# A Strassen-Winograd matmul on one core: the first region's last turn as quarter products, measures later, b21's stores behind VectorE

## The chip, the core and the metric

The kernel runs on one core of a Trainium2 chip. A core has TensorE (matrix products into PSUM, eight banks of 128 x 512 float32), VectorE, ScalarE, GpSimd (POOL) and SyncE (SP), each with an instruction queue of its own that runs in order; they meet through semaphores. Data moves between HBM and SBUF by DMA; DMAs are issued here from the queues of SP, ScalarE and POOL. POOL's loads also turn float32 into float16 on the way. The metric is the device time of one execution in microseconds (us); the time given for a kernel is the median over its runs.

## The reference

```python
def setup_inputs():
    m, k, n = 4096, 4096, 4096
    return {
        "a": np.random.randn(m, k).astype(np.float32),
        "b": np.random.randn(k, n).astype(np.float32),
        "alpha": np.float32(0.01),
    }

def reference(a, b, alpha):
    x = np.matmul(a, b)
    return np.where(x > 0, x, alpha * x)
```

## The kernel before

**Tiling.** The output is 16 regions of 1024 x 1024: row group g and column block j, each from 0 to 3. A region's rows are halves h = 0, 1 of 512 rows (MT = 4 tiles of 128), its columns halves nt = 0, 1 of 512. K = 4096 is four units u of 1024 (KC = 8 chunks of 128); units 0, 1 are the first half of K, units 2, 3 the second. So a region multiplies a 2 x 2 block matrix a11, a12, a21, a22 by b11, b12, b21, b22. Every element of a and b is rounded to float16.

**A region after the first** (the loop at L819, in the order of `regions`: (0, 1), (0, 2), (0, 3), then (1, 2), (1, 0), (1, 3), (1, 1), and so on) takes Winograd's seven products instead of eight. `PRODUCTS` (L684) lists their operands: a11 b11, a12 b21, s2 t2, s3 t3, s1 t1, a22 (b21 less t2), s4 b22. The sums s1 to s4 of a (`sum_a`, L598) and the sums t of b (`b_sum`, L618) are made by VectorE in float16. A plain product is 64 matmuls of 128 x 512 (`product`, L838); it goes through k first, so that it reads the first unit of a half before the second. The result of product 0 in banks `y` is copied by ScalarE into banks `z` (L1258); product 1 is added into `z`, product 2 into `y`, product 3 goes into new banks.

**Quarters.** In later groups some products are themselves taken with seven products of quarters: `quarter_product` (L781) is 16 matmuls of 256 columns. Their sums of quarters are made by `sums_of_a` and `sums_of_b` on VectorE. Where two results share the start of a sum, ScalarE copies the bank that holds it to another one.

**The first region** (0, 0) is plain: eight steps of 64 matmuls, in turns by `TURNS` (L35), `[[0], [0, 1], [1, 2, 3], [2, 3]]`: half h = 0 with unit 0, half 1 with units 0, 1, half 0 with units 1, 2, 3, and last half 1 with units 2, 3. Each step `i` of the loop at L464 fetches what the next step needs, runs its matmuls into eight banks, turns the next pieces of a (VectorE transposes, L143), and, at a turn's end, adds the banks to `part[h]` in SBUF (`spill`, L322). `leave_first` (L333) applies the leaky step and stores. `at[0, 0, 0]`, the first unit of a, is brought in by TensorE transposes and copies (L380 to L387), and is laid out plainly; all other a tiles hold pairs of chunks.

**What stands around the change, in the order of the program.** At step 5's end VectorE makes the last turn's a22 (eight transposes) and the spills of `part[0]`, then four leaky steps, which let SP store `part[0]`. The loads of the next region's b11 and b12 are issued by POOL at step 5. In the loop for region (0, 1): POOL's loads of b21, b22 (L1197), POOL's stores of `part[1]`, VectorE's s1 and s2, product 0, copies of `y` to `z`, four b sums (L1276, L1279), the end of a measure, `keep_half` (SP stores the float16 b21 for later groups), s3, product 1.

**Buffers.** The pool `x` has three slots, through which pass in turn the first loads, `room`, `part[0]`, `part[1]`, then s1, s2 of region (0, 1); a new tile waits until all readers and writers of the slot's last tile are through. `b21` and the like have two slots each (two units), `a16` three.

**Measures** (`Measure`, L222) collect sums of squares of a and b by row and column for a check of the scale at the end: ScalarE squares four pieces of 2048 (L237), VectorE adds and folds them (L246 to L271). In the kernel before, the measure of a21 and those of the first columns' b21 and b22 are taken in the first region's last turn.

**What b is kept.** A b unit that a later group needs again is stored in float16 (`kept_half`) and loaded from there by SP (L561). The order on each queue is that of the program (`manual_schedule`, L88).

Of the kernel before, what the change touches and what calls it, by code (L numbers as in the profile page):

```python
# [8 lines left out]
P = 128  # L9
# [28 lines left out]
OTHERS = (0, 3)  # L38
KEPT_T = {CACHED: 1, 0: 2, 3: 2}


# [8 lines left out]
def kernel(  # L50
# [154 lines left out]

    def plain(t):
        return t.rearrange("p c m e -> p (c m e)").rearrange("p (c m) -> p c m", c=KC)

    def a_cols(t, c, mt, is_plain=False):
        rows = slice(mt * P, (mt + 1) * P)  # L210
        return plain(t)[:, c, rows] if is_plain else t[:, c // 2, rows, c % 2]

# [59 lines left out]

    class MeasureFirst(Measure):


        def end(self):
            for pairs, n in ((False, 0), (True, 2)):
                if n:
                    self.square(3)
                total = self.held[n]  # L280
                nc.vector.tensor_add(total, total, self.held[n + 1])
                fold(self.which, total, self.held[n + 1], pairs, 2.0)

    def halves(t):
# [4 lines left out]
    def mm(ps, h, u, mt, nt, c, first, last):  # L289
        nc.tensor.matmul(  # L290
            ps, a_cols(at[0, h, u], c, mt, (h, u) == (0, 0)), bt[0, u, nt][:, c, :],
            start=first, stop=last,
        )
# [39 lines left out]
    def leave_first(h, mt):  # L333
        kept = part[h][:, mt, :]
        leaky(kept)
        row = (h * MT + mt) * P
        if h == 0:
            nc.sync.dma_start(out[row:row + P, :2 * NT], kept)
        else:
            stores.append((out[row:row + P, :2 * NT], kept))  # L340

# [24 lines left out]
    def turn_a(i, r, tiles):  # L366
        k = slice(r * rw, (r + 1) * rw)
        shared = r and tiles == 1
        if shared and i == MT - 1:
            turned = both.pop()  # L370
        else:
            tag = "ps7" if r else f"ps{4 + i}"
            turned = psum_pool.tile([P, per, 2 if r else 1, P], DT, name="turned", tag=tag)
        if shared and i < MT - 1:
            both.append(turned)
        cols = a_rounded[:, :, k].rearrange("m t (p c) -> m t c p", c=per)
        for t in range(tiles):
# [9 lines left out]
        copy(to, turned)  # L387
# [31 lines left out]
    for n, (what, i, *more) in enumerate(order):  # L419
# [22 lines left out]
    room = x_pool.tile([P, 4, KC // 2 * RM], BF16, name="room", tag="x")  # L442
    part[0] = x_pool.tile([P, MT, 2 * NT], FP32, name="part", tag="x")
# [12 lines left out]
    for fetch in fetches[2]:  # L456
# [4 lines left out]
        Measure(1, halves(bt[0, 0, nt]) + halves(bt[0, 1, nt]), False, places)  # L461
        for nt, places in enumerate((room, c_rooms))]

    for i in range(1, len(steps)):  # L464
        t, h, u, first, last = steps[i]
# [24 lines left out]
        for g, (todo, leaves) in enumerate(groups):  # L490
            for mt, c in todo:
                for nt in range(2):
                    mm(banks[mt, nt], h, u, mt, nt, c, first and c == 0, last and c == KC - 1)
            if i == 5 and g > 1:
                spill(t, h, leaves, banks)
            for piece, turn in enumerate(following):
                if where[piece] == g:
                    turn()
            if leaves is not None and (i != 5 or g == 1):
                spill(t, h, leaves, banks)  # L500
            if leaves is not None and t and i != 5:
                leave_first(h, leaves)
# [9 lines left out]
        if i == 5:  # L512
            first_measure = Measure(0, halves(at[0, 1, 0]) + halves(at[0, 1, 1]), True, room)
            first_measure.begin()
            last_columns = [
                Measure(1, halves(bt[0, 2, nt]) + halves(bt[0, 3, nt]), False, places)
                for nt, places in enumerate((room, c_rooms))]
            for n in range(4):
                last_columns[1].square(n)
        if i == 6:  # L520
            first_measure.end()
            for n in range(4):
                last_columns[0].square(n)


    last_columns[0].end()

# [20 lines left out]
    def fetch_unit(i, u, nt, later=False):  # L548
# [9 lines left out]
        elif g and j == CACHED:  # L558
            nc.sync.dma_start(t, rows_of(kept[nt], u, 0, KC, True))
        elif half and (g and j == LAST or g > 1 and j in OTHERS):  # L560
            nc.sync.dma_start(t.rearrange("p c n -> p (c n)"), kept_half[j][u - 2, nt])  # L561
# [11 lines left out]
    whole_s = {}  # L573
    first_a = at[0, 0, 0]

    def flat(t):
        if t is first_a:
            return plain(t).rearrange("p (c e) m -> p c m e", e=2)
        return t.rearrange("p c m e -> p (c m e)")

    def like(t, other):

        return t if other is first_a else t.rearrange("p c m e -> p (c m e)")

    def a_sum(to, x0, x1, op):
        if x0 is first_a or x1 is first_a:
            f = lambda t: flat(t) if t is first_a else t
        else:
            f = flat
        nc.vector.tensor_tensor(f(to), f(x0), f(x1), op)  # L590
# [31 lines left out]
    def measure(i, which, x, y):  # L622
# [5 lines left out]
        parts = halves(tiles[0]) + halves(tiles[1])  # L628
        if tiles[0] is first_a:
            return MeasureFirst(which, parts, None)  # L630
        return Measure(which, parts, not which)
# [15 lines left out]
    def judge(line):  # L647
# [40 lines left out]

    HALF = NT // 2
    QUARTER = KC * HALF  # L690
    kept_s2 = dram_pool.tile([2, P, KC * RM], DT, name="kept_s2")
# [32 lines left out]

    def sums_of_a(g, name, room, some=(1, 2, 3, 4), made=None):

# [13 lines left out]
        make(2, 1, (0, 0), SUB)  # L740
        make(3, (0, 0), (1, 0), SUB)
        make(4, (0, 1), 2, SUB)

# [69 lines left out]
    def next_a(g, h, half):  # L813
        made = [p for k in range(2) for p in pieces_a(g, h, 2 * half + k)]
        return made

    in_quarters = False
    Y, Z = [4, 5, 6, 7], [0, 1, 2, 3]
    for i, (g, j) in enumerate(regions):  # L819
# [12 lines left out]

        def keep_half(some=(0, 1)):
            for nt in some:
                for k in ks:
                    nc.sync.dma_start(kept_half[j][k, nt], B(1, nt, k).rearrange("p c n -> p (c n)"))

        def product(n, banks, first):  # L838
# [23 lines left out]
            for mt, k, c in order:  # L862
                t = operand(g, name, k)
                nc.tensor.matmul(  # L864
                    banks[mt], a_cols(t, c, mt, t is first_a), B(half, nt, k)[:, c, :],
                    start=first and (k, c) == todo[0], stop=(k, c) == todo[-1], skip_group_check=not first,
                )
# [327 lines left out]
        if i == 0:  # L1195
# [4 lines left out]
            sum_a(g, "s1")  # L1200
            sum_a(g, "s2")
        coming = {}
        if turning:
# [52 lines left out]
        if not in_first:  # L1256
            for mt in range(MT):
                nc.scalar.copy(z[mt], y[mt])  # L1258
        if second_of_group:
            sums_of_a(g, "s1", new_a16)  # L1260
# [55 lines left out]
        if final:  # L1316
            good = next(judged)
        if (g, j) == (0, LAST):
            keep_half((1,))
        for k in [] if in_fourth else ks[1:] if turning and g else ks:  # L1320
# [16 lines left out]
        if in_fourth:  # L1337
            s5[3] = t[:, 3]
            load_sums("s1", s5, (3,))
            if g == 1 and j in OTHERS:  # L1340
                keep_half((1,))
        if turning and g:
# [132 lines left out]
        if not in_quarters:  # L1475
# [4 lines left out]
            else:  # L1480
                add(u2[::-1], z[::-1])
        if turning:

# [116 lines left out]
```

## Time and profile before

| what | value |
|---|---|
| median of 3 runs | 1523.87 us (1522.62 to 1524.34) |
| profiled execution | 1520.24 us |
| its span, first to last instruction | 1518.4 us |
| mean granted TensorE clock | 0.998 |
| DMA queue of POOL's loads (q0) | 45.1% of 16 engines' span |
| chain that ended last, TensorE's lines | L787 28%, L864 21%, L845 9% |

All times in a profile's rows are us from the span's start. A row of a timeline has its start, its length, the engine, the line and operation, written tile and read tiles, the shape and how many were merged; in brackets stands the idle time before it and what ended it. PE is TensorE's matmuls, PEld its weight loads, DVE VectorE, ACT ScalarE; a queue that issues a DMA has a q behind its name. The length of a merged row of matmuls counts the pipeline's depth once, so products are best measured from start to start.

### The profile page before, as it was taken

How to read it: one execution, taken by the hardware profiler on the slowest of the kernel's cores; microseconds unless marked ns; L12 is line 12 of the kernel's file. 1: busy time of each engine (PE TensorE's matmuls, PEld its weight loads, DVE VectorE, ACT ScalarE, POOL GpSimd, SP SyncE). 2: the span in 40 equal slices, each digit the busy share in tenths (PEclk: the TensorE clock that was granted, in tenths of full speed). 3: DMA queues.
4: the chain of work that ended last, by engine and by line, in shares of the span. 5: the costliest groups of instructions: out<-in, count | busy, mean ns of one | idle time of the engine just before them, and what ended most of it. 6: DMA issues, size and time to landing. Idle time of an engine off the chain costs nothing.

```text
span 1518.4 us, 24421 instructions
## 1 busy us (share of the span) xinstructions
PE 1507.9 (99%) x9883; PEld 965.8 (64%) x9883; DVE 1200.9 (79%) x1250; ACT 524.6 (35%) x906; POOL 252.2 (17%) x418
## 2 busy tenths in 40 slices
PE   9999999999999999999999999999999999999998
PEld 4444444444445667485544688888454488888887
DVE  4588966786696597697779698987887876998797
ACT  2441435647411123225671122323574112242322
POOL 5632110134201102012330101000331000100000
PEclk9999999999999999999999999999999999999999
DMA  9999697899889999999898989979989697987845
GB/s 245 188 219 259 151 278 212 129 220 192 202 347 228 299 293 296 282 289 300 199 246 344 261 315 257 345 246 316 242 215 306 258 278 278 242 291 188 348 154 183
DMA packets 193965, 384.97 MB, mean 254 GB/s; under 512 B 17585, under 2 KB 126385, under 8 KB 178738
## 3 DMA queue, kind: packets, MB, share of 16 engines
q0 software_dynamic: 115584, 108.03, 45.1%
q1 hardware_dynamic: 71058, 245.53, 43.1%
q10 hardware_dynamic: 7200, 29.76, 5.0%
q8 instruction: 79, 1.29, 0.3%
q14 instruction: 44, 0.36, 0.1%
HBM read 359.66 MB, written 129.50 MB: 322 GB/s over the span
## 4 chain that ended last, share of the span: by engine, by line
PE 58%; DVE 0%; issue 0%
PE ps L787 28%; PE ps L864 21%; PE ps L845 9%; DVE c L1146 0%; DVE b L620 0%; DVE c L320 0%
## 5 line engine op out<-in xcount | busy, mean ns | idle before, releaser
L864 PE MATMUL ps<-b,a 128*128 128x512 f16 x1984 | 433.3, 380 | 2.2 <-DVE a L590 2.2
L864 PEld LDWEIGHTS <-a 128*128 128x128 f16 x1984 | 194.4, 98 | 237.0 <-DVE a L590 2.7
L864 PE MATMUL ps<-b,s 128*128 128x512 f16 x1472 | 321.5, 379 | 0.5 <-DVE b L620 0.5
L864 PEld LDWEIGHTS <-s 128*128 128x128 f16 x1472 | 144.1, 98 | 173.9 <-issue 0.8
L564 POOL DMA_DIRECT2D b<-in_b_dram x120 | 88.9, 746 | 860.9 <-PE ps L787 282.6
L787 PEld LDWEIGHTS <-q 128*128 128x128 f16 x2192 | 214.1, 98 | 25.8 <-issue 0.4
L620 DVE TENSOR_TENSOR b<-b 128x4096 f16<-128x4096 f16 x82 | 185.8, 2285 | 42.5 <-DMA b<-in_b_dram 32.6
L887 ACT COPY c<-ps 128x512 f32<-128x512 f32 x164 | 86.2, 595 | 294.3 <-PE ps L864 157.0
L143 DVE STREAM_TRANSPOSE a<-a 128x512 uint32<-128x512 uint32 (+2 forms) x120 | 127.0, 1105 | 65.1 <-DMA a<-in_a_dram 64.6
L134 POOL DMA_DIRECT2D a<-in_a_dram x252 | 137.4, 552 | 246.7 <-ACT junk L639 74.9
L787 PEld LDWEIGHTS <-a 128*128 128x128 f16 x1440 | 140.9, 98 | 17.4
L320 DVE SCALAR_TENSOR_TENSOR c<-c 128x1024 f32<-128x1024 f32 (+2 forms) x123 | 141.8, 1190 | 8.9 <-ACT c L887 8.6
L639 ACT ACTIVATE junk<-a 128x512 bf16<-128x512 f16 x192 | 121.2, 631 | 69.9 <-DMA a<-in_a_dram 64.7
L787 PE MATMUL ps<-b,q 128*128 128x256 f16 x1088 | 128.1, 273 | 0.0
L237 ACT ACTIVATE sq<-b 128x2048 bf16<-128x2048 f16 x56 | 104.0, 1911 | 59.6 <-DVE sq L246 53.5
L787 PE MATMUL ps<-q,q 128*128 128x256 f16 x1024 | 119.0, 273 | 0.0
L290 PE MATMUL ps<-b,a 128*128 128x512 f16 x512 | 112.2, 379 | 0.3
L787 PE MATMUL ps<-b,a 128*128 128x256 f16 x912 | 107.4, 273 | 0.0
L787 PEld LDWEIGHTS <-s 128*128 128x128 f16 x960 | 93.9, 98 | 11.4
L290 PEld LDWEIGHTS <-a 128*128 128x128 f16 x512 | 49.7, 98 | 60.6 <-issue 1.4
L892 DVE TENSOR_TENSOR c<-ps,c 128x512 f32<-128x512 f32 x76 | 47.0, 679 | 30.4 <-PE ps L864 30.4
L845 PE MATMUL ps<-b,a 128*128 128x256 f16 x640 | 70.7, 273 | 0.0
(148 smaller groups left out, 1386.5 us busy)
## 6 DMA issues: line engine op xcount, KB each, us to landing
b<-in_b_dram POOLq DMA_DIRECT2D x128, 512.0 KB, 13.1
out_dram<-c SPq DMA_DIRECT2D x118, 512.0 KB, 8.0
a<-in_a_dram POOLq DMA_DIRECT2D x244, 128.0 KB, 5.5
b<-kept_half SPq DMA_DIRECT2D x28, 1024.0 KB, 12.4
b<-kept SPq DMA_DIRECT2D x20, 1024.0 KB, 8.4
q<-kept_qs ACTq DMA_DIRECT2D x40, 512.0 KB, 7.6
s<-kept_s SPq DMA_DIRECT2D x18, 1024.0 KB, 7.1
q<-kept_qs SPq DMA_DIRECT2D x28, 512.0 KB, 6.8
```

The costliest lines, as they stand in the source:

```text
L134: nc.gpsimd.dma_start(a16[32 * q:32 * q + 32], src.rearrange("(g i) w -> i g w", i=32))
L143: nc.vector.transpose(part.rearrange("p c m e -> p c (m e)").bitcast(U32) .rearrange("p c (g i) -> p g c i", i=32), src[:, :, i * n:(i + 1 ...
L237: nc.scalar.activation(to, self.parts[n], SQUARE)
L290: nc.tensor.matmul(ps, a_cols(at[0, h, u], c, mt, (h, u) == (0, 0)), bt[0, u, nt][:, c, :], start=first, stop=last,)
L320: nc.vector.scalar_tensor_tensor(t, t, alpha, t, op0=MULT, op1=MAX if alpha <= 1 else MIN)
L564: nc.gpsimd.dma_start(t[:, c:c + 4, :], b_rows(j, u, c, 4, nt, g > 0))
L620: nc.vector.tensor_tensor(f(to), f(x0), f(x1), op)
L639: nc.scalar.activation(junk, piece[:, q, :], SQUARE, accum_out=to[:, 4 * n + q:4 * n + q + 1])
L787: nc.tensor.matmul(to[m], xq[:, c // 2, rows, c % 2], yq[:, c, :], start=first and c == 0 and m < banks, stop=c == KC - 1, skip_group_chec ...
L845: nc.tensor.matmul(to, a_cols(operand(g, name, k), c, q // 2 * 2 + m), B(half, nt, k)[:, c, q % 2 * HALF:(q % 2 + 1) * HALF], start=False, ...
L864: nc.tensor.matmul(banks[mt], a_cols(t, c, mt, t is first_a), B(half, nt, k)[:, c, :], start=first and (k, c) == todo[0], stop=(k, c) == t ...
L887: nc.scalar.copy(to, bank)
```

## The change

The first region's last turn (steps 6 and 7) is taken out of the loop and written as two products of quarters, one for each nt, interleaved (`leave_in_quarters`). The sums of b21's quarters for nt = 0 are made at step 4's end, in `room`. In each set, the product of a22's last quarter by t4 needs no sum of a22 and goes ahead of those that do. `part[1]` gets the blocks by additions from PSUM; the leaky steps of both parts stand at the end, `part[0]`'s between the additions of the two nt.

```diff
+KEPT_IN = {(LAST, 0): 0, (LAST, 1): 0, (0, 0): 1, (0, 1): 1, (3, 0): 1, (3, 1): 0}
...
-    for i in range(1, len(steps)):
+    for i in range(1, len(steps) - last_turn):
...
-            if i == 5 and g > 1:
+            if i == 5 and 1 < g < MT:
                 spill(t, h, leaves, banks)
...
-        if i == 5:
-            for mt in range(MT):
-                leave_first(h, mt)
...
+            q = quarters_of_first(0)
+            f = lambda n: t_of_b21[n].rearrange("p (c n) -> p c n", n=HALF)
+            nc.vector.tensor_tensor(f(3), q[1, 1], q[0, 1], SUB)
+            nc.vector.tensor_tensor(f(2), f(3), q[0, 0], ADD)
+            nc.vector.tensor_tensor(f(4), q[1, 0], f(2), SUB)
...
+    def leave_in_quarters():
...
+        chain, one, other, shared, fourth = [new_bank(0), new_bank(2)], [new_bank(1), new_bank(3)], [], [], []
+        for nt in range(2):
+            quarter_product(x[0, 0], b[nt][0, 0], into(chain[nt]), True)
+            nc.scalar.copy(one[nt], chain[nt])
+        for nt in range(2):
+            quarter_product(x[0, 1], b[nt][1, 0], into(one[nt]))
+        fourth.append(new_bank(4))
+        quarter_product(x[1, 1], t(0, 4), into(fourth[0]), True)
+        tt(fx(1), xf[1, 0], xf[1, 1], ADD)
+        tt(fx(2), fx(1), xf[0, 0], SUB)
+        more(0, 0, 0, one[0])
+        tt(t(0, 1), b[0][1, 1], t(0, 2), SUB)
+        quarter_product(sx(2), t(0, 2), into(chain[0]))
+        other.append(new_bank(5))
+        nc.scalar.copy(other[0], chain[0])
+        shared.append(new_bank(1))
+        quarter_product(sx(1), t(0, 1), into(shared[0]), True)
+        tt(fx(3), xf[0, 0], xf[1, 0], SUB)
+        quarter_product(sx(3), t(0, 3), into(chain[0]))
+        tt(fx(4), xf[0, 1], fx(2), SUB)
+        quarter_product(sx(4), b[0][1, 1], into(other[0]))
+        tt(t(1, 3), b[1][1, 1], b[1][0, 1], SUB)
+        new_t(2, t(1, 3), b[1][0, 0], ADD)
+        quarter_product(sx(2), t(1, 2), into(chain[1]))
+        spill(2, 0, MT - 1, banks)
+        other.append(new_bank(6))
+        nc.scalar.copy(other[1], chain[1])
+        new_t(1, b[1][1, 1], t(1, 2), SUB)
+        shared.append(new_bank(7))
+        quarter_product(sx(1), t(1, 1), into(shared[1]), True)
+        more(1, 0, 0, one[1])
+        fourth.append(new_bank(3))
+        quarter_product(sx(3), t(1, 3), into(chain[1]))
+        nc.scalar.copy(fourth[1], chain[1])
+        quarter_product(sx(4), b[1][1, 1], into(other[1]))
+        new_t(4, b[1][1, 0], t(1, 2), SUB)
+        quarter_product(x[1, 1], t(1, 4), into(fourth[1]))
+        for nt in range(2):
+            more(nt, 1, 1, chain[nt])
+            for r in (1, 0):
+                more(nt, r, 1, shared[nt])
+            if nt == 0:
+                more(nt, 1, 0, chain[nt])
+            more(nt, 0, 1, other[nt])
+            more(nt, 1, 0, fourth[nt])
+            if nt == 0:
+                for mt in range(MT):
+                    leave_first(0, mt)
+        for mt in range(MT):
+            leaky(part[1][:, mt, :])
+            row = (MT + mt) * P
+            stores.append((out[row:row + P, :2 * NT], part[1][:, mt, :]))
...
-    Y, Z = [4, 5, 6, 7], [0, 1, 2, 3]
+    Y, Z = [2, 3, 6, 7], [0, 1, 4, 5]
```

Here `more` is one VectorE addition of a bank (128 x 512) to a block of `part[1]`, `tt` a VectorE operation on two tensors of 128 x 2048, `new_t` the same into a new slot of `a16`.

The measures move: a21's begins in region (0, 1) ahead of product 0 and ends behind the b sums; the first columns' b21 is measured in region (1, 0), ahead of its products, and their b22 in (3, 0).

```diff
     EARLY = {
-        (1, 3): [B11], (1, 1): [B11], (2, 3): [B21], (2, 1): [B12], (3, 1): [B21],
+        (1, 0): [B21], (1, 3): [B11], (1, 1): [B11], (2, 3): [B21], (2, 1): [B12], (3, 1): [B21],
     }
+    IN_C = (3, 0)
...
+            first_measure = Measure(0, halves(at[0, 1, 0]) + halves(at[0, 1, 1]), True)
+            first_measure.begin()
...
+        in_c = (g, j) == IN_C
+        if in_c:
+            m = measure(i, *B22)
+            m.room = [c_pool.tile([P, 2048], BF16, name="sq", tag=f"c{n}") for n in (side, side, 1 - side, 1 - side)]
+            for n in range(4):
+                m.square(n)
+        if second_of_group:
+            in_other = lambda n: c_pool.tile([P, QUARTER], DT, name="sums", tag=f"c{1 - side}") if n == 4 else new_a16()
+            sums_of_a(g, "s1", in_other if g == 1 else new_a16, m.end if in_c else None)
```

The stores of b for later groups follow a table, with b22 of column block 3 stored in group 0 instead of loaded again in group 1. In group 0, b21's stores get a one-column copy on VectorE in front of them.

```diff
-        def keep_half(some=(0, 1)):
-            for nt in some:
-                for k in ks:
-                    nc.sync.dma_start(kept_half[j][k, nt], B(1, nt, k).rearrange("p c n -> p (c n)"))
+        def keep_half(nt, behind=False):
+            for k in ks if KEPT_IN.get((j, nt)) == g else ():
+                t = B(1, nt, k).rearrange("p c n -> p (c n)")
+                if behind:
+                    nc.vector.tensor_copy(t[:, :1], t[:, :1])
+                nc.sync.dma_start(kept_half[j][k, nt], t)
...
         if i == 0:
-            last_columns[1].end()
+            first_measure.end()
...
-        if g == 1 and j in OTHERS or (g, j) == (0, LAST):
-            keep_half((0,))
+        keep_half(0, not g)
         note_rows()
         if first_of_group:
             sum_a(g, "s3")
...
         product(1, z, False)
...
+        if not g and i:
+            keep_half(1)
```

The first unit of a gets the layout of the others: its copies out of PSUM write pairs of chunks, and the plain layout's special cases (`plain`, `flat`, `like`, `MeasureFirst`) go.

```diff
-        to = plain(a0)[:, r * per:(r + 1) * per, first * P:(i + tiles) * P]
-        turned = turned.rearrange("p c t m -> p c (t m)")
+        to = a0[:, r * per // 2:(r + 1) * per // 2, first * P:(i + tiles) * P, :].rearrange("p c m e -> p c e m")
+        turned = turned.rearrange("p (c e) t m -> p c e (t m)", e=2)
```

More of the change, by code (lines that the diff above doesn't have):

```diff
@@ L271, in fold @@
             nc.vector.tensor_tensor(stats[:, n, which], stats[:, n, which], r, op)
[L273 to L282, printed above, removed]
     def halves(t):
@@ L336, in leave_first @@
         row = (h * MT + mt) * P
[L337 to L340, printed above, removed]
+        nc.sync.dma_start(out[row:row + P, :2 * NT], kept)
     runs = RUNS[0]
@@ L573 @@
     whole_s = {}
[L574 to L583, printed above, removed]
     def a_sum(to, x0, x1, op):
[L586 to L589, printed above, removed]
+        f = lambda t: t.rearrange("p c m e -> p (c m e)")
         nc.vector.tensor_tensor(f(to), f(x0), f(x1), op)
@@ L723, in sums_of_b, with sums_of_a @@
             tt(f(1), y[1, 1], f(2), SUB)
-    def sums_of_a(g, name, room, some=(1, 2, 3, 4), made=None):
+    def sums_of_a(g, name, room, ahead_of_4=None, some=(1, 2, 3, 4), made=None):
         x = {key: q.rearrange("p c m e -> p c (m e)") for key, q in quarters_of_a(g, name).items()}
@@ L815, in next_a, with t, new_t, more @@
         return made
+    def leave_in_quarters():
+        x = quarters_of_a(0, "a22")
+        xf = {key: by_chunk(q) for key, q in x.items()}
+        sums = {n: c_pool.tile([P, QUARTER], DT, name="sums", tag=f"c{n % 2}") for n in range(1, 5)}
+        sx = lambda n: a_quarter(sums[n])
+        fx = lambda n: by_chunk(sums[n])
+        b = [quarters_of_first(nt) for nt in range(2)]
+        t_of_b22 = {}
+        tt = nc.vector.tensor_tensor
+        def t(nt, n):
+            if (nt, n) == (1, 3):
+                return b[1][0, 1]
+            return b_quarter(t_of_b22[n] if nt else t_of_b21[n])
+        def new_t(n, x0, x1, op):
+            t_of_b22[n] = new_a16()
+            tt(t(1, n), x0, x1, op)
+        def more(nt, r, n, bank):
+            cols = slice(nt * NT + n * HALF, nt * NT + (n + 1) * HALF)
+            block = part[1][:, 2 * r:2 * r + 2, cols]
+            nc.vector.tensor_add(block, pair(bank), block)
+        chain, one, other, shared, fourth = [new_bank(0), new_bank(2)], [new_bank(1), new_bank(3)], [], [], []
[50 more added lines that the diff above has]
+            stores.append((out[row:row + P, :2 * NT], part[1][:, mt, :]))
```

52 lines of the change are left out of this document (19 added, 33 removed).

## The prediction

> **What bounds the kernel now.** I read the page first, then the waits of TensorE, then the timelines of TensorE and VectorE around the end of the first region, and the other engines where the change touches them.
>
> ```profile
> span 1518.4 us, 24421 instructions
> PE 1507.9 (99%) x9883; PEld 965.8 (64%) x9883; DVE 1200.9 (79%) x1250; ACT 524.6 (35%) x906; POOL 252.2 (17%) x418
> ```
> ```profile
> PE ps L864 <- DVE a L590: 2.2, 1, 2.2
> PE ps L864 <- DVE b L620: 0.5, 1, 0.5
> ```
> ```profile
> 120.77 27.79 PE L864 MATMUL ps<-b,a 128*128 128x512 f16 x128
> 148.40 13.98 PE L864 MATMUL ps<-b,s 128*128 128x512 f16 x64
> 164.55 15.68 PE L864 MATMUL ps<-b,a 128*128 128x512 f16 x64 [2.17 <-DVE a L590]
> 180.06 13.98 PE L864 MATMUL ps<-b,s 128*128 128x512 f16 x64
> ```
> ```profile
> 164.60:166.00 1.40, 1.40 (x6) 0.74 0.00 0
> 166.00:168.00 2.00, 2.00 (x6) 0.50 0.00 0
> 168.00:170.00 2.00, 2.00 (x9) 0.83 0.63 232
> ```
>
> TensorE is the bound. Beyond the first 15 us it waits twice; the 2.17 us wait for s3 (L590) in the region behind the first one is the larger. In the windows behind it (sum, mean busy, granted clock) the clock fell to a half, so that product took 15.68 us and not 13.98: 1.70 us more. That one wait costs 2.17 + 1.70 = 3.87 us.
>
> From 120.77 to 148.40 lie two products: 27.63 us, 13.82 each. The last turn is as many matmuls, so it began at 120.77 - 27.63 = 93.14. The second product of the next region (the one with b21) began at 134.59.
>
> **The last turn, part by part.** A quarter product is the gap between these two starts:
>
> ```profile
> 483.95 1.91 PE L787 MATMUL ps<-b,a 128*128 128x256 f16 x16
> 485.70 3.66 PE L787 MATMUL ps<-q,q 128*128 128x256 f16 x32
> ```
>
> 1.75 us. Fourteen take 24.5 us in place of 27.63, so TensorE saves 3.1 us if it is fed. The next region's products then fall due at 117.64 and 131.46. What feeds them, and what comes behind, is VectorE's queue, which runs in program order:
>
> ```profile
> 81.35 0.34 DVE L271 TENSOR_TENSOR stats<-stats,r 128x16 f32<-128x16 f32 x3
> 86.82 2.12 DVE L143 STREAM_TRANSPOSE a<-a 128x512 uint32<-128x512 uint32 x2 [5.12 <-DMA a<-in_a_dram]
> 91.44 2.44 DVE L331 TENSOR_TENSOR part<-ps,part 128x512 f32<-128x512 f32 x4
> 96.98 2.09 DVE L143 STREAM_TRANSPOSE a<-a 128x512 uint32<-128x512 uint32 x2
> 100.15 4.62 DVE L320 SCALAR_TENSOR_TENSOR part<-part 128x1024 f32<-128x1024 f32 x4
> 104.69 1.22 DVE L246 TENSOR_TENSOR room<-room 128x2048 bf16<-128x2048 bf16 x1
> 111.33 0.34 DVE L271 TENSOR_TENSOR stats<-stats,r 128x16 f32<-128x16 f32 x3
> 129.78 4.48 DVE L590 TENSOR_TENSOR s<-a,a 128x4096 f16<-128x4096 f16 x2
> 134.18 6.62 DVE L590 TENSOR_TENSOR s<-s,a 128x4096 f16<-128x4096 f16 x2
> 149.06 4.67 DVE L620 TENSOR_TENSOR b<-b,b 128x4096 f16<-128x4096 f16 x2 [3.58 <-DMA b<-in_b_dram]
> ```
> ```profile
> L719 DVE TENSOR_TENSOR q<-b 128x2048 f16<-128x2048 f16 x36 | 44.0, 1221 | 6.8 <-PE ps L864 5.2 <-DVE b L713 0.5
> ```
>
> The three sums of b21 that are moved ahead (3 x 1.22 = 3.7) fit into the 5.12 us that VectorE sat idle before 86.82; without that cover they delay everything behind them by up to 3.7. The last transpose of a22 ends at 99.07, and the new list starts there. It keeps ahead of TensorE by little: the second sum of a is made at 99.07 + 2 x 1.22 = 101.5 and is due behind five quarter products, at 93.14 + 8.75 = 101.9. I cost the last turn's own stalls at 0, between 0 and 1 us; the next paragraph shows why they hardly count.
>
> **The new wait.** In the first region behind it, the change puts a copy of one column of b21 onto itself on VectorE ahead of each store of b21. It stands in VectorE's program behind s1, s2, the four sums of b and the end of the moved measure. The second product reads b21, and its first matmul reads that very column: it must wait for a write that now comes ahead of it. Before, it needed the load alone. Does a write of one element hold a whole transfer in this kernel? It does, SyncE waited for a 128x1 memset of s2, and I take it that the program's order of reads and writes is kept for TensorE in the same way:
>
> ```profile
> SPq L806 <- DVE s L805: 49.3, 8, 19.2
> L805 DVE MEMSET s<- 128x1 f16 x9 | 0.5, 59 | 0.0
> ```
>
> VectorE's list from 99.07 to the copies, by the rows above: nine sums of 2048 at 1.22 = 11.0; fifteen additions out of PSUM (two spills, two early, eleven at the end) at 2.44/4 = 0.61, with gaps 0.63, = 9.4; eight leaky steps at 4.62/4 = 9.2; s1 and s2, four at 4.48/2, = 9.0; the b sums, four at 4.67/2, = 9.3; the measure 6.9 (104.69 to 111.6 for the same one) and 0.65 for its fourth square, which now comes late, by the next row, = 7.6; the copies 2 x 0.06 by the memset.
>
> ```profile
> 185.29 1.23 DVE L250 TENSOR_TENSOR sq<-sq 128x2048 bf16<-128x2048 bf16 x1 [0.65 <-ACT sq L237]
> ```
>
> That is 55.6, so 154.7. The b sums also need b22, whose last piece landed at 149.06. Its issue:
>
> ```profile
> 114.08 2.97 POOL L564 DMA_DIRECT2D b<-in_b_dram  x4 [16.78 <-PE ps L290]
> 121.25 2.23 POOL L564 DMA_DIRECT2D b<-in_b_dram  x3 [4.21 <-issue]
> 123.76 0.74 POOL L564 DMA_DIRECT2D b<-in_b_dram  x1 [0.28 <-DMA b<-in_b_dram]
> ```
> ```profile
> 101.39 3.74 SPq L338 DMA_DIRECT2D out_dram<-part  x4
> 128.67 13.03 SPq L836 DMA_DIRECT2D kept_half<-b  x2
> ```
> ```profile
> q0 software_dynamic: 16037, 17.09, 97.9%
> ```
>
> 25.3 us from issue to landing, in a queue busy 97.9% of the time from 60 to 160. Its buffer is now let go by the thirteenth quarter product at 93.14 + 22.75 = 115.9, so it is issued near 118 and, by the same 25.3, lands near 143.3. In its way stand the four output stores of L338, now from about 118; out of its way is the first b21 store, now behind. The ends are no wait (142.4, when VectorE gets there) and 149.06 as before; I take 143.0, 0.6 us of wait. So the copies are done at **155.3**, and TensorE, ready at 131.46, waits 23.9 us. Behind that matmul stand all of TensorE's queue, and then ScalarE's copies of the product and their stores. No part of VectorE's list waits for this product, so it is a stall and no deadlock. The 3.1 us of the quarters are swallowed: the list on VectorE, not TensorE, sets the time.
>
> The product starts at 155.4 in place of 134.59: **+20.8**. The clock falls again; the row behind 164.55 prices the return at **+1.7** (0 to 2 as ends). While TensorE stands, VectorE gets ahead: s3 follows from 155.3 and its first half is there near 157.6, wanted at 155.4 + 1.7 + 27.6 = 184.7. The wait for s3 and its slow clock go: **-3.87**. Sum: +18.6.
>
> The TensorE page of the Trainium skill, "TensorE: Matmul & The Clock Gate", Part 1, lets the clock halve only after an idle window of about 3.4 us. By that the old 2.17 us wait would have cost no clock, the credit would be 2.2 and the sum +20.3; the windows at 0.74 and 0.50 decide against it here.
>
> **The layout.** a0's halves become pairs like the other a tiles.
>
> ```profile
> L590 DVE TENSOR_TENSOR s<-s,a x2: 2279/3346/4414, 134.2 to 138.5; 128x4096 f16<-128x4096 f16 x2
> L387 DVE COPY a<-turned x2: 690/691/692, 13.2 to 15.4; 128x1024 f16<-128x1024 f16 x2
> L387 ACT COPY a<-turned x4: 578/585/586, 6.1 to 8.7; 128x512 f16<-128x512 f16 x4
> ```
>
> It removes 4414 - 2279 = 2.1 us from s2 and as much from s3 (counted above). It makes the six copies at the start write with gaps. If that doubles VectorE's two as it doubled the sum, 2 x 0.5 to 0.7; ends 0 and 1.4 at the start. That cannot reach the end: the loads pace VectorE up to 86.82, and the list from 99.07 sets the new wait. I take 0. "VectorE: DVE Perf Modes" of the Trainium skill, on Mode 2x_1P, asks for steps of one element for two results in a cycle: it speaks against this edit, the trace agrees with 4414 against 2279, and by it the start takes the upper end, 1.4 us, with the sum as it stands; whether ScalarE's copies suffer, no run here shows.
>
> **Moved measures, stores.** b21's measure of the first columns goes into region (1, 0), ahead of its copies for the second product:
>
> ```profile
> 518.75 1.06 ACT L1258 COPY ps<-ps 128x512 f32<-128x512 f32 x2 [9.07 <-PE ps L864]
> 525.22 1.23 DVE L736 TENSOR_TENSOR q<-s,q 128x2048 f16<-128x2048 f16 x1 [5.99 <-DMA kept_qs<-q]
> b<-in_b_dram POOLq DMA_DIRECT2D x2, 512.0 KB, 19.8
> ```
>
> ScalarE idled 9.07 us and VectorE 5.99 there. b21's second half lands about 494.9 + 19.8 = 514.7 (two loads issued from 494.8); the last two squares at 1.9 end near 519 and the copies follow by 520, before 522.2. Cost 0. The measure in (3, 0) stands where no copies are, b22's stores and loads on SyncE's queue have no TensorE wait behind them, and the first region's stores on that queue are due only when s2 takes part's buffer: 0 for each, 0 to 1 together.
>
> **The forecast** is 1523.87 + 18.6 = 1542.5. The profiled execution took 1520.24 (its span and 1.84), 3.63 less than the median; on its own time the sum is 1538.8. A measurement of this kernel tells 0.2%, 3.0 us, from no change.
>
> **The rivals.**
> *Not held.* The copies don't hold the second product: TensorE goes through at 131.46, s3 is there at 157.6, before 159.1, and both gains stay: 1523.87 - 3.1 - 3.9 = 1516.9, up to 1518.3 with the layout's start. It decides where VectorE reaches the copies by 131.5, or the column is not counted as written. Against it: 24 us are missing, and L805's row. 0.08.
> *b22 lands as late as before.* At 149.06: + 4.67 + 7.6 + 0.1 = 161.4, 6.1 later: 1548.6. For it: the busy queue and the stores moved into its way; against: six us earlier issue. 0.14.
> *ScalarE late in (1, 0)*, on top of the stall. With 26.7 us to land (the longest of b's tile from 505 on, in the row below) b21 is there at 521.6, two squares and a copy end at 526, and the product due at 522.2 waits 4 us and loses 1.7 of clock: 1548. Against: 19.8 in the row above. 0.08.
>
> ```profile
> DMA to landing us min/median/max: 9.8/18.1/26.7
> ```
>
> **How the numbers follow.** The forecast has 0.70, and its own range is 1540 to 1546 (1 us of spacing in the list, up to 2 of clock, 1 of stalls). The whole range, 1537 to 1550, takes in the second and third rival and leaves the first and about as much of odd cases outside. Faster 0.08 (the first rival), same 0.01, slower 0.91.
>
> **What would show it.** In the changed kernel's waits, TensorE's first row at L864 (its new number) is a wait of some 24 us for VectorE's copy of b; the s3 wait is gone; quarter products in the last turn at 1.75 each, the next region's first product near 117.6; VectorE's one-column copies near 155; granted clock near 0.5 behind them. The prediction is wrong if the second product starts near 131, if VectorE's list between the last transpose and the copies is not some 56 us, or if TensorE is held elsewhere.

## The result, and the profile after

The changed kernel takes 1550.24 us (median of 6, 1545.98 to 1551.70); the kernel before 1521.90 (median of 6). The ratio is 1.018, 95% interval 1.0163 to 1.0197: 27 us slower. The sign was as forecast, and so were the place and the mechanism of the largest part; the size was forecast as 18.6 us, and two losses elsewhere were not in that sum. The measured time lies outside the forecast's own range (1540 to 1546) and 0.24 us above the end of its whole range (1537 to 1550). The profiled executions are 1548.19 and 1520.24, 27.95 apart.

The page's first lines and TensorE's waits in the changed kernel (waited-for, us in total, times, longest):

```profile
span 1546.3 us, 24631 instructions
PE 1507.3 (97%) x9979; PEld 975.5 (63%) x9979; DVE 1213.0 (78%) x1261; ACT 528.4 (34%) x911; POOL 249.3 (16%) x414
```
```profile
PE ps L908 <- DVE b L879: 23.3, 1, 23.3
PE ps L908 <- ACT ps L1304: 3.5, 1, 3.5
PE ps L908 <- DMA b<-in_b_dram: 3.1, 3, 1.7
```

TensorE works as long as before (1507.3 against 1507.9 us) and waits longer. L879 is the one-column copy, L908 the plain products' matmul, L1304 ScalarE's copies y to z. s3's wait is gone. TensorE's timeline of the changed kernel, from the last turn on:

```profile
94.61 7.15 PE L750 MATMUL ps<-b,a 128*128 128x256 f16 x64
117.52 1.91 PE L750 MATMUL ps<-q,a 128*128 128x256 f16 x16
119.26 13.98 PE L908 MATMUL ps<-b,a 128*128 128x512 f16 x64
156.57 15.39 PE L908 MATMUL ps<-b,a 128*128 128x512 f16 x64 [23.33 <-DVE b L879]
171.80 13.98 PE L908 MATMUL ps<-b,s 128*128 128x512 f16 x64
199.43 13.98 PE L908 MATMUL ps<-b,s 128*128 128x512 f16 x64
560.70 13.98 PE L908 MATMUL ps<-b,s 128*128 128x512 f16 x64
654.66 13.98 PE L908 MATMUL ps<-b,s 128*128 128x512 f16 x64
```

Of the kernel before two more starts are needed, the first from TensorE's timeline, the second from the chain that ended last:

```profile
536.03 13.98 PE L864 MATMUL ps<-b,s 128*128 128x512 f16 x64
```
```profile
627.08 13.97 PE ps L864 x64
```

| start of | before | after | shift |
|---|---|---|---|
| the last turn (before: worked out in the prediction) | 93.14 | 94.61 | +1.5 |
| region (0, 1), first product | 120.77 | 119.26 | -1.5 |
| second product (before: worked out) | 134.59 | 156.57 | +22.0 |
| third product | 148.40 | 171.80 | +23.4 |
| fifth product | 180.06 | 199.43 | +19.4 |
| region (1, 0), third product | 536.03 | 560.70 | +24.7 |
| region (1, 3), third product | 627.08 | 654.66 | +27.6 |
| the span | 1518.4 | 1546.3 | +27.9 |

So 19.4 us were lost by the fifth product, where the forecast had 18.6, and two further losses of 5.3 and 2.9 us, in (1, 0) and (1, 3), came where it had 0.

VectorE's list in the changed kernel, its last transpose, its later pieces and the copies:

```profile
87.33 1.23 DVE L504 TENSOR_TENSOR room<-b,room 128x2048 f16<-128x2048 f16 x1
88.69 2.10 DVE L144 STREAM_TRANSPOSE a<-a 128x512 uint32<-128x512 uint32 x2
98.85 2.10 DVE L144 STREAM_TRANSPOSE a<-a 128x512 uint32<-128x512 uint32 x2
122.11 3.40 DVE L803 TENSOR_TENSOR part<-ps,part 128x512 f32<-128x512 f32 x5
134.37 4.49 DVE L554 TENSOR_TENSOR s<-s,a 128x4096 f16<-128x4096 f16 x2
144.33 4.68 DVE L584 TENSOR_TENSOR b<-b,b 128x4096 f16<-128x4096 f16 x2 [0.79 <-DMA b<-in_b_dram]
156.36 0.21 DVE L879 COPY b<-b 128x1 f16<-128x1 f16 x2
```

From the last transpose's end at 100.95 to the product's start at 156.57 are 55.6 us. The list between them has the pieces that were added up (nine sums, fifteen additions out of PSUM, eight leaky steps and so on), and it began 1.9 us later.

### The profile page after: what moved, and what is told of

It reads as the page before. It is cut to its first block, busy times and chain, and to the rows that moved or that the text cites. A ratio compares the mean times of both kernels' runs of the same rounds, so it can differ in the third digit from the quotient of the medians.

```text
span 1546.3 us, 24631 instructions
## 1 busy us (share of the span) xinstructions
PE 1507.3 (97%) x9979; PEld 975.5 (63%) x9979; DVE 1213.0 (78%) x1261; ACT 528.4 (34%) x911; POOL 249.3 (16%) x414
## 4 chain that ended last, share of the span: by engine, by line
PE 85%; DMA 9%; DVE 3%; POOL 1%; issue 1%; ACT 0%; SPq 0%; DVEq 0%; ACTq 0%
PE ps L908 45%; PE ps L750 30%; PE ps L889 9%; DMA b<-in_b_dram 8%; DMA a<-in_a_dram 1%; PE ps L276 1%; DVE a L144 0%; POOL a L135 0%; POOL b L195 0%; DMA a_in<-in_a_dram 0%; DVE b L584 0%; DVE part L803 0%; DVE part L317 0%; POOL b L542 0%; DVE q L798 0%
## 5 line engine op out<-in xcount | busy, mean ns | idle before, releaser
L908 PE MATMUL ps<-b,a 128*128 128x512 f16 x1984 | 435.5, 381 | 30.0 <-DVE b L879 23.3
L908 PEld LDWEIGHTS <-a 128*128 128x128 f16 x1984 | 194.9, 98 | 266.1 <-DVE b L879 23.8
L908 PE MATMUL ps<-b,s 128*128 128x512 f16 x1472 | 321.5, 379 | 0.0
L908 PEld LDWEIGHTS <-s 128*128 128x128 f16 x1472 | 144.0, 98 | 173.3
L584 DVE TENSOR_TENSOR b<-b 128x4096 f16<-128x4096 f16 x82 | 185.7, 2286 | 30.4 <-DMA b<-in_b_dram 18.9
L750 PEld LDWEIGHTS <-a 128*128 128x128 f16 x1536 | 150.3, 98 | 18.7
L234 ACT ACTIVATE sq<-b 128x2048 bf16<-128x2048 f16 x60 | 111.5, 1910 | 62.7 <-DVE sq L243 44.9
L750 PE MATMUL ps<-b,a 128*128 128x256 f16 x976 | 114.5, 273 | 0.0
L750 PEld LDWEIGHTS <-s 128*128 128x128 f16 x960 | 93.9, 98 | 11.4
L276 PE MATMUL ps<-b,a 128*128 128x512 f16 x384 | 84.5, 379 | 1.6 <-DVE a L370 0.7
L889 PE MATMUL ps<-b,a 128*128 128x256 f16 x640 | 70.7, 273 | 0.0
L889 PE MATMUL ps<-b,s 128*128 128x256 f16 x640 | 70.7, 273 | 0.0
L889 PEld LDWEIGHTS <-s 128*128 128x128 f16 x640 | 62.6, 98 | 7.2
```

The source lines that it names most:

```text
L234: nc.scalar.activation(to, self.parts[n], SQUARE)
L276: nc.tensor.matmul(ps, a_cols(at[0, h, u], c, mt), bt[0, u, nt][:, c, :], start=first, stop=last,)
L750: nc.tensor.matmul(to[m], xq[:, c // 2, rows, c % 2], yq[:, c, :], start=first and c == 0 and m < banks, stop=c == KC - 1, skip_group_chec ...
L889: nc.tensor.matmul(to, a_cols(operand(g, name, k), c, q // 2 * 2 + m), B(half, nt, k)[:, c, q % 2 * HALF:(q % 2 + 1) * HALF], start=False, ...
L908: nc.tensor.matmul(banks[mt], a_cols(t, c, mt), B(half, nt, k)[:, c, :], start=first and (k, c) == todo[0], stop=(k, c) == todo[-1], skip_ ...
```

## The experiments

Two theories stood at first. **The hold:** the copy writes a column that the second product reads, so the product waits until VectorE, in program order, has made it. **The rival:** b21 or another transfer is late there, or VectorE's list holds the product in some other way, and the copy only stands at that place. Times are set against the kernel before as ratios, since its own median moved by up to 2 us between the sets of runs (1521.3, 1520.5, 1519.7).

**No copy.**

```diff
-        keep_half(0, not g)
+        keep_half(0)
```

> The changed kernel without the one-column copy ahead of b21's stores. Theory (the copy holds the second product): the 23.3 us wait goes and its 1.6 us of slow clock with it, the second product starts near 133.1 instead of 156.6; 1550.2 - 24.9 = 1525.3. b21's stores come early again and may push b22 back from 144.3 towards 149, then s3 comes near 161 where it is due at 160.7, up to 2 us more. Rival (b21 or VectorE's list is late for another reason, the copy only stands at that place): a wait of 15 us or more stays at the second product, 1540 or more.

1526.36 us, 1.0036 of before (1.0025 to 1.0048): 22 us less than the changed kernel, where 24.9 were expected. The wait is gone; what is left in this region is mainly s3's, since b22 now came near 149.3 (VectorE's wait for it):

```profile
119.03 27.79 PE L908 MATMUL ps<-b,a 128*128 128x512 f16 x128
163.74 15.54 PE L908 MATMUL ps<-b,a 128*128 128x512 f16 x64 [2.58 <-DVE a L554]
```
```profile
149.36 4.68 DVE L584 TENSOR_TENSOR b<-b,b 128x4096 f16<-128x4096 f16 x2 [6.69 <-DMA b<-in_b_dram]
```

The first two products run through in one row. The stores' cost without a copy is seen as well: s3 is 2.6 us late, because b22 landed 5 us later than in the changed kernel. Of these 5 us, up to 3 may be chance: in the profiled executions of the kernels below whose stores stand behind VectorE's list, b22 landed between 144.9 and 147.3; it landed at 149.4 here and at 150.4 in the other kernel that issues them early (the copy ahead of the b sums).

**The copy behind the product.**

```diff
-        keep_half(0, not g)
+        if g:
+            keep_half(0)
...
         product(1, z, False)
+        if not g:
+            keep_half(0, True)
```

> The changed kernel with the copy and b21's stores moved in program order from ahead of the second product to behind it. Theory: the copy now follows the matmuls that read the column, nothing holds TensorE, b21's stores still go behind VectorE's list: second product near 133.1, b22 near 144, no wait for s3, 1525.3 and not above the kernel without the copy. Rival (late stores or VectorE's list hold the product, not the order of write and read): the wait stays, 1540 or more.

1523.70 us, 1.0015 (1.0004 to 1.0027). The instructions are the same, only write and read have changed places, and there is no wait in this region, neither for the copy nor for s3. 1.018 - 1.0015 is 25 us, as expected. TensorE's waits in this kernel after the start:

```profile
PE ps L908 <- DMA b<-in_b_dram: 3.6, 2, 2.1
PE ps L908 <- ACT ps L1304: 2.8, 1, 2.8
```

**The last column in place of the first.**

```diff
-                    nc.vector.tensor_copy(t[:, :1], t[:, :1])
+                    nc.vector.tensor_copy(t[:, -1:], t[:, -1:])
```

> The changed kernel with the copy on the last column of each b21 unit instead of the first. Theory in its narrow form (only matmuls that read the written column wait): of the first unit's matmuls 28 pass, 16 for the first four chunks and 12 for the next three, 28 x 0.216 = 6.0 us, so TensorE stops near 139.1 and the wait is 17.4 us; 1550.2 - 6.0 = 1544.2. Wide form (any write into the tile holds every read of it): no difference, 1550.2.

1542.87 us, 1.0139 (1.0115 to 1.0163): 6.2 us less than the changed kernel, 6.0 expected. TensorE stops inside the product now:

```profile
159.52 5.64 PE L908 MATMUL ps<-b,a 128*128 128x512 f16 x14 [20.23 <-DVE b L879]
```

It stopped at 159.52 - 20.23 = 139.3, where 139.1 was forecast; b22 landed later in this execution than in the profiled one of the changed kernel (147.3 against 144.3), so the copies came at 159.3 and the wait was 20.2 and not 17.4. With b22's landing moving the time by 3 us, that the medians differ by nearly the 6.0 expected is in part luck; the place where TensorE stopped is not. The hold follows the column: the 28 matmuls that don't read it went through, and the first that reads it waited.

**The kernel before with the copy alone.** Its loop in `keep_half`:

```diff
+                    t = B(1, nt, k).rearrange("p c n -> p (c n)")
+                    if not g and not nt:
+                        nc.vector.tensor_copy(t[:, :1], t[:, :1])
```

> The kernel before with nothing but the one-column copy ahead of b21's first stores. Theory: VectorE reaches the copies at 160.1 by the old trace, 3 us sooner if b22 lands sooner with the stores out of its way, so the second product starts at 157.3 to 160.3 instead of 134.6 (+22.7 to +25.7), + 1.6 clock, - 3.9 for the s3 wait that goes: +20.4 to +23.4, 1542 to 1545 against 1521.9. Rival (it takes the quarters or the moved measures): no change, 1522.

1541.07 us, 1.0134 (1.0116 to 1.0152), 20.4 us above before:

```profile
156.38 15.28 PE L867 MATMUL ps<-b,a 128*128 128x512 f16 x64 [21.88 <-DVE b L838]
```

The copy alone, without the rest of the change, makes most of its loss.

**The copy ahead of the b sums.** `keep_half(0, True)` moved up VectorE's list, still ahead of the product:

```diff
         if middle:
             middle.begin()
+        if not g:
+            keep_half(0, True)
```

> The changed kernel (1550.2) with the one-column copies and b21's stores moved ahead of the four sums of b on VectorE, behind s2; they still stand ahead of the second product. Theory (the hold lasts until VectorE's list reaches the copies): VectorE is there at 138.8 instead of 156.4, the second product starts near 139 and waits 6 us instead of 23.3; 17.4 less, 1532.8. The stores come earlier and may push b22 and the b sums back by up to 5 us, which s3 can bear. Rival (the length of the wait is that of a transfer, not of VectorE's list): 20 us or more of wait stay, 1547 or more.

1528.47 us, 1.0063 (1.0039 to 1.0087), 17.8 us less than 1.018. The wait is as long as VectorE's list up to the copies:

```profile
138.75 0.21 DVE L879 COPY b<-b 128x1 f16<-128x1 f16 x2
```
```profile
138.96 15.63 PE L908 MATMUL ps<-b,a 128*128 128x512 f16 x64 [5.74 <-DVE b L879]
```

That settles the hold. The other two losses were not in the forecast's sum. What was thought of them was: ScalarE's squares of b21 in (1, 0) stand ahead of its copies and wait for b21's loads; and in (1, 3) b22's loads of what was stored (`kept_half`, the float16 b in HBM) pass b21's. The next four kernels start from the one with the copy behind the product.

**b21 not measured in (1, 0).**

```diff
-        (1, 0): [B21], (1, 3): [B11], (1, 1): [B11], (2, 3): [B21], (2, 1): [B12], (3, 1): [B21],
+        (1, 3): [B11], (1, 1): [B11], (2, 3): [B21], (2, 1): [B12], (3, 1): [B21],
```

> The kernel with the copy behind the second product (1523.7, 1.0015 of before), less the measure of the first columns' b21 in region (1, 0), which is left out. Theory: ScalarE's squares, each waiting for b21 to land, stand ahead of its copies y to z and held TensorE 2.8 us and 1.6 us of slow clock; both go, 1519.3 or 0.9985 of before. Rival (the copies are late by the DMAs or VectorE whatever is measured): the wait for ScalarE stays, 1523.7.

1521.23 us, 1.0000 (0.9989 to 1.0012). The wait for ScalarE is gone, but 2.3 us came back and not 4.4: a wait for the b sums that it had covered took its place at the third product, and the wait for b21 in (1, 3) stayed.

```profile
532.92 13.97 PE L908 MATMUL ps<-b,s 128*128 128x512 f16 x64 [1.90 <-DVE b L584]
620.74 8.66 PE L908 MATMUL ps<-b,a 128*128 128x512 f16 x32 [3.42 <-DMA b<-in_b_dram]
```

**b22 of block 3 loaded raw** (in float32 from `b`, by POOL, as in the kernel before).

```diff
-... (3, 0): 1, (3, 1): 0}
+... (3, 0): 1, (3, 1): 1}
```

> The kernel with the copy behind the second product, but b22 of column block 3 is loaded from b by POOL in group 1 again and stored there, as before. Theory: its loads from the store on SyncE's queue overtook b21's loads on POOL's and cost TensorE 3.6 us of waits in region (1, 3); these go, 1520.1 or 0.9991, and the wait for ScalarE in (1, 0) stays. Rival (b21 is late there because VectorE's delay in (1, 0) moved the stores of b into its way): the waits for b21 stay at 3 us or more, 1523.7; by the same theory they go in the kernel without the measure.

1514.37 us, 0.9951 (0.9935 to 0.9967): 9.7 us less than with the store, where 3.6 was expected, and the fastest of all. (The waits and the slow clock in the profiled execution with the store, 2.8 + 1.4 + 3.6, make 7.8 of it; the rest lies within the intervals.) Both waits went, the one for ScalarE too, against what was expected. After the start there are these waits left:

```profile
PE ps L276 <- DVE a L144: 0.8, 1, 0.8
PE ps L908 <- DVE b L584: 0.2, 1, 0.2
```

So one table entry of the change carried both. It stores b22 in group 0 and loads it from there in group 1; the next run keeps the first half alone.

**Stored, not loaded.**

```diff
-        elif half and g > KEPT_IN.get((j, nt), G):
+        elif half and g > KEPT_IN.get((j, nt), G) and (g, j, nt) != (1, 3, 1):
```

> The kernel with the copy behind the second product (1523.7); b22 of column block 3 is still stored in group 0, but in group 1 it is loaded from b by POOL and not from the store. Theory: the store at 389 pushes a's loads and with them VectorE's stores 5 us back, b21 of (1, 0) lands 2 to 3 us late and ScalarE's copies behind its squares hold TensorE 2.8 us and 1.6 us of slow clock; this stays. The load from the store is what overtakes b21's loads in (1, 3); those 3.6 us go: 1520.1, 0.999 of before. Rival (the store has no part in it, both waits hang on the load): both waits go, 1515, as in the kernel without either (1514.4).

1519.35 us, 0.9992 (0.9980 to 1.0003), as expected. The wait for b21 in (1, 3) is gone, the one for ScalarE is there:

```profile
520.00 16.88 PE L908 MATMUL ps<-b,a 128*128 128x512 f16 x64 [3.33 <-ACT ps L1304]
```

The load of the stored b22 makes the wait in (1, 3), the early store the one in (1, 0). That one needs the squares ahead of ScalarE's copies as well: it went when b21 was not measured there, and it went when b22 was not stored early.

**b21's measure behind ScalarE's copies**, together with b22 loaded raw:

```diff
-        ... ([], early) if in_first or have_t2 else (early[:1], early[1:])
+        ... ([], early) if in_first or have_t2 or (g, j) == (1, 0) else (early[:1], early[1:])
```

> The kernel with the copy behind the second product, b22 of block 3 loaded by POOL again, and b21's measure in (1, 0) begun behind ScalarE's copies instead of ahead of them; all that is computed stays. Theory: 1523.7 less 4.4 less 3.6 is 1515.7, 0.9962 of before, if the squares fit behind the copies. If they delay ScalarE's copies of the second product instead, a wait of 1 to 5 us appears at the fourth product of (1, 0) and 1517 to 1521 comes out.

1522.27 us, 1.0006 (0.9996 to 1.0016), 8 us worse than with the measure where the change has it, and just outside the 1517 to 1521 of the worse case. The wait at the fourth product came, but not by way of ScalarE's copies. VectorE's additions of the measure now stand between two pairs of its b sums, the last square waits for them, and the b sums behind them (L584) come only at 545.64; TensorE waits for these, and pays more than was to be saved:

```profile
537.53 1.91 ACT L234 ACTIVATE sq<-b 128x2048 bf16<-128x2048 f16 x1 [11.36 <-DVE sq L243]
```
```profile
536.27 1.22 DVE L243 TENSOR_TENSOR sq<-sq 128x2048 bf16<-128x2048 bf16 x1
545.64 4.68 DVE L584 TENSOR_TENSOR b<-b 128x4096 f16<-128x4096 f16 x2
```
```profile
550.38 3.21 PE L750 MATMUL ps<-b,s 128*128 128x256 f16 x16 [5.59 <-DVE b L584]
```

**The kernel before with the layout alone**: the copies' rearrangement and `a_cols` as in the change, and the special cases of the plain layout gone.

> The kernel before with nothing but the layout of a's first unit as pairs. Theory: at the start TensorE waits 0.7 us more for VectorE's copies out of PSUM and another 0.6 for a round of b behind them; s2 and s3 become 2.1 us shorter each, so the wait for s3 of 2.17 us and 1.7 us of slow clock go: -3.9 + 0.7 to 1.5, 1518.9 to 1519.7 where before is 1522, 0.998 to 0.999. If the start costs more than it brings, 1.000 or above.

1518.80 us, 0.9986 (0.9976 to 0.9996), 2.1 us gained, within what was expected, though not in the way: the wait for s3 is 1.51 us, not gone, but it no longer costs clock. The start costs 0.7 us for VectorE's copies and 0.6 for b, as expected; the wait for the copies:

```profile
17.34 104.77 PE L290 MATMUL ps<-b,a 128*128 128x512 f16 x484 [0.74 <-DVE a L387]
165.07 13.99 PE L862 MATMUL ps<-b,a 128*128 128x512 f16 x64 [1.51 <-DVE a L590]
```

## Why the prediction was right, and where it was short

**The hold** was right in kind, place and size: 23.9 us forecast, 23.3 measured, VectorE's list 56.2 us forecast (99.07 to 155.3) and 55.6 measured. The kernels without the copy and with the copy behind the read, the one with the last column and the one with the copy higher in the list show that it is the order of write and read, and that VectorE's list sets its length. The rival "not held" falls.

**The quarters** save what was said on TensorE: 94.61 to 119.26 are 24.65 us, 24.5 forecast. Under the hold nothing of it is seen, as forecast.

**b22** was wanted at 143.5 and came at 144.3, a wait of 0.8 us where 0.6 was forecast; the second rival (149.06) didn't come. That it was so near is in part luck: in profiled executions of other kernels with the stores behind VectorE's list b22 came at 144.9 (stored, not loaded), 147.0 (copy behind the product) and 147.3 (last column). Up to 3 us of the size hang on it.

**The clock's return** was taken at 1.70 and cost 156.57 to 171.80 less 13.82, 1.41 us.

**The layout.** The step "that cannot reach the end" failed. VectorE's two copies went from 691 to 1302 ns, as allowed for, and the last turn began 1.5 us late; b21's last piece, its sums and the transposes behind them came later with it (86.82 became 88.69), and the whole list with them. It was taken that the loads pace VectorE there whatever the start does; the loads moved too. The kernel with the layout alone shows it: there the next region begins 1.2 us later than before (121.95 against 120.77), and the same transposes wait for a's loads until 88.59:

```profile
88.59 2.11 DVE L143 STREAM_TRANSPOSE a<-a 128x512 uint32<-128x512 uint32 x2 [5.47 <-DMA a<-in_a_dram]
```

So the three sums of b21 that were moved ahead did fit into this wait, as forecast.

**Moved measures and stores** is the step that made most of the miss: "Cost 0" for the measure in (1, 0), and 0 for b22's stores and loads. Both were wrong, and by the prediction's own last sign, TensorE held elsewhere, this part of it was wrong.

First, ScalarE in (1, 0): the forecast took 19.8 us for b21's second half to land, the median of two loads, where the last piece counts. In the changed kernel it was issued at 514.26 in two loads, and the last square could begin 28.6 us later:

```profile
537.64 1.91 ACT L234 ACTIVATE sq<-b 128x2048 bf16<-128x2048 f16 x1 [2.62 <-DMA b<-in_b_dram]
542.82 1.91 ACT L234 ACTIVATE sq<-b 128x2048 bf16<-128x2048 f16 x1 [3.27 <-DMA b<-in_b_dram]
```

TensorE's next product then waited for ScalarE:

```profile
545.27 15.59 PE L908 MATMUL ps<-b,a 128*128 128x512 f16 x64 [3.52 <-ACT ps L1304]
```

3.52 us of wait and 1.6 of clock. That was the third rival, priced at 4 and 1.7 and given 0.08. What made it happen was not looked at: the 2 MB store of b22 in (0, 3). With it (the kernel with the copy behind the product) VectorE waits 5.9 us for a's loads at the turn to group 1, and the stores of quarter sums leave 5 us later; without it (b22 loaded raw) VectorE has no such wait there. The fourth square with the store, then without it:

```profile
517.90 1.91 ACT L234 ACTIVATE sq<-b 128x2048 bf16<-128x2048 f16 x1 [3.49 <-DMA b<-in_b_dram]
```
```profile
515.52 1.91 ACT L234 ACTIVATE sq<-b 128x2048 bf16<-128x2048 f16 x1 [1.70 <-DMA b<-in_b_dram]
```

With the store it begins 2.4 us later, though the loads were issued 0.7 us earlier (490.03 against 490.75). Without it the square began 24.8 us after the issue, 5 us more than the 19.8 of the forecast, and still TensorE did not wait: a "Cost 0" would have held without the store, though not by the sum that gave it. VectorE's wait with the store, then the stores of the first quarter sums with it and without it:

```profile
404.79 2.12 DVE L144 STREAM_TRANSPOSE a<-a 128x512 uint32<-128x512 uint32 x2 [5.89 <-DMA a<-in_a_dram]
```
```profile
454.38 4.31 SPq L698 DMA_DIRECT2D kept_qs<-q  x4
```
```profile
449.42 4.32 SPq L698 DMA_DIRECT2D kept_qs<-q  x4
```

That the store causes the wait is shown by the two runs together, the one that stores and doesn't load, and the one that does neither; that it does so by way of the later stores is argued from these rows and was not tried by itself.

Second, b22's loads from the store: "no TensorE wait behind them" looked at their own queue alone. In (1, 3) they stand beside b21's loads on POOL's queue. POOL issued b21's last four at 608.39, SyncE b22's two from 616.68. The loads of each, with their median time to landing:

```profile
b<-in_b_dram POOLq DMA_DIRECT2D x4, 512.0 KB, 34.1
```
```profile
b<-kept_half SPq DMA_DIRECT2D x2, 1024.0 KB, 8.8
```

b22, wanted later, landed within 9 us; b21 took 34. TensorE waited 3.1 us for it. The same four loads in the kernel with b22 loaded raw, where nothing stood beside them from the store:

```profile
b<-in_b_dram POOLq DMA_DIRECT2D x4, 512.0 KB, 26.4
```

So the sum was right where VectorE's list was added up piece by piece, and short by 8.2 us where a measure and a transfer were set to nothing because no wait stood directly behind them. That the whole range ended only just below the measured time is luck: its upper end was set for b22 landing late or ScalarE late, one of them at a time, and no rival had the loss in (1, 3).

**What the change is worth** without the hold and without b22's early store: 0.9951 (0.9935 to 0.9967), 7 us faster than before. The layout by itself, on the kernel before, brought 2.1 us. What the quarters, the moved measures and the later stores of b21 each bring was not taken apart.

## What to carry to other kernels

A column written in place to order something behind it is a write for every reader of that column that follows in the program: put it behind the last reader that must not wait, or tie the order to a tile that nobody else reads (this second way was not tried here). When an edit puts a write ahead of a read, add up the writing engine's whole list up to that write; here that gave the wait within 1 us. And a transfer that is moved or put on another queue can be paid for by the transfers beside it: ask which load it passes and who waits for the last piece of that load.

## What the runs showed of the hardware

The clock's loss did not grow with the wait: 1.41 us after 23.3 idle, 1.70 after 2.17, 1.6 after 3.52, and 2.9 in one execution after 3.33 (16.88 against 13.98); waits of 1.51 and 1.90 cost none (13.99, 13.97), and nor did one of 2.12 with the copy behind the product, where the granted clock stayed at 1.00:

```profile
626.62 3.61 PE L908 MATMUL ps<-b,a 128*128 128x512 f16 x16 [2.12 <-DMA b<-in_b_dram]
```

The Trainium skill, "TensorE: Matmul & The Clock Gate", Part 1, has the clock fall after a window of about 3.4 us without work; in these runs the shortest wait with a loss behind it is 2.17 us and the longest without one 2.12. The granted clock behind the long wait, by windows of the changed kernel (length, busy time of TensorE, weight loads, VectorE, ScalarE and POOL, clock, DMA share, GB/s):

```profile
156.50:158.00 1.50, 1.43 (x4) 0.59 (x5) 1.50 (x3) 0.00 (x0) 0.00 (x0) 0.50 0.44 180
158.00:160.00 2.00, 2.00 (x8) 0.72 (x6) 2.00 (x2) 0.00 (x0) 0.00 (x0) 0.64 1.06 426
160.00:162.00 2.00, 2.00 (x11) 0.91 (x10) 0.97 (x1) 0.00 (x0) 0.00 (x0) 1.00 0.96 401
```

ScalarE's copies out of PSUM are slower too when they write with gaps, if less than VectorE's: 734 ns against 585 for 512 elements, where VectorE's went from 691 to 1302 for 1024.

```profile
L370 ACT COPY a<-turned x4: 732/734/742, 6.3 to 9.0; 128x512 f16<-128x512 f16 x4
L370 DVE COPY a<-turned x2: 1302/1302/1302, 13.5 to 16.3; 128x1024 f16<-128x1024 f16 x2
```

And in (1, 3) loads that turn float32 into float16 on POOL's queue took 34 us to land beside plain loads on SyncE's that took 9, though they were issued at least 5 us earlier (608.4 to 611.4 against 616.7 and later); without these plain loads they took 26.
